# Attention values products: low parts of probabilities against 64 columns of weights, in another order

## The chip, the cores and the metric

The kernel runs on one core of a Trainium2 chip. The metric is the device time of one execution in microseconds (us). A difference under 0.2% (some 3 us here) can't be told from none.

Five engines work side by side: TensorE (PE, whose weight loads the profile shows apart as PEld), VectorE (DVE), ScalarE (ACT), GpSimd (POOL) and SyncE (SP, which issues most transfers).

## The reference

Two token sequences, of 2048 and of 512 tokens with 1024 channels, each go through one attention layer, one Fourier mixing layer and a last normalisation, in float32. Only the end of the attention layer matters here. For each block of 128 queries, with the keys of the block itself and of its two neighbours and a band of 128 to either side:

```
scores = jnp.where(mask, q @ k / 8 + bias, -inf)
p = jnp.exp(scores - m)
denom = jnp.sum(p, -1) + jnp.exp(sink - m)
o = (p / denom) @ v
```

There are 16 heads of 64 channels in 4 groups. Four heads share one group's keys and values.

## The kernel before

Each operand of a product is held as a high part (float32 rounded to a shorter mantissa, `fp32r` in the profile) and a low part (what is left), and a product a·b is made as high·high, high·low and low·high.

The work is in five chunks of 512 tokens (chunk 0 is the short sequence, chunks 1 to 4 the long one). Each chunk makes its keys and values, and then goes through 8 pairs of heads. In it, queries, gates and the output projection of the pairs are made between the attention steps of other pairs, in an order written out by hand: the tables `PERIOD` (chunks 1 to 4) and `FIRST` (chunk 0). Each table is one period, and a period handles two query blocks of one head pair. All TensorE instructions of this stage are chained into that one order.

Names that matter:

- `S1`, `S2` (line 650): scores of a block into the PSUM tiles `spt`. `T0`, `T1` (line 709): transposes of the normalised probabilities into `tp`.
- `hi0`, `hi1` (line 722, ACT) and `lo0`, `lo1` (line 726, DVE): high and low parts of the transposed probabilities, into the tile `pts`. Its second index tells the part: 0 is high, 1 is low.
- `AV1`, `AV2` (lines 759 to 770, function `half`): the values products, into the PSUM tile `av`, one bank for each of the two query blocks. The weights are the values `v`: 128 columns, 64 of the high part and then 64 of the low part. The moving operand is `pts`. So the upper 64 partitions of `av` get what the low parts of the values give, and the lower 64 what the high parts give. `t2` (line 787) copies the upper 64, `add` (line 797) adds them to the lower.

The keys of a block are split in an upper and a lower half of 64 rows, and each half is a product of its own: 64 rows of TensorE's array, 128 columns. `half` issues one product for rows 0 to 63 and one for rows 64 to 127 in turn. The two go to different banks, and TensorE runs them beside each other. In `AV1` rows 0 to 63 work for the first block and rows 64 to 127 for the second, in `AV2` the other way round. Between the two stand the transposes `T0`. `AV2` waits, by an instruction made in `swapped` (line 526), until the other rows are done with its bank.

What a half of the rows does for one block is listed in `reached` (line 741): three key blocks (0 the one before, 1 the block itself, 2 the one behind) times two parts. Of one of the outer key blocks (`edge`) these 64 keys reach only 64 of the 128 queries because of the band, so that product has 2x64 moving columns: a narrow product. The others have 256 (two heads of 128 queries): wide products. At the ends of a sequence a key block is missing, and so are its products. The last two blocks of a chunk's last head pair go another way (line 775) that the change doesn't touch.

Of the kernel before, what the change touches and what calls it, by code (L numbers as in the profile page):

```python
# [20 lines left out]
P = 128  # L21
# [34 lines left out]
def encoder(  # L56
# [17 lines left out]
    av = spsum.tile([P, 2, 512], F32, name="av")  # L74
# [126 lines left out]
    def pe(ins):  # L201
        return seq(PE, ins) if PE in chain else ins

    def attention_phase():

        with ExitStack() as es:
# [167 lines left out]
            vblk, k_splits = {}, []  # L374
# [151 lines left out]
            def swapped(places):  # L526

                before = []
                for last, h in places:
                    if last[1 - h] is not None:  # L530
                        before.append(last[1 - h])
                        last[1 - h] = None
                if before:
                    wait = pe(PE.nop())
                    for ins in before:
                        tc.add_manual_dep(wait.ins, ins.ins.name, DONE, reason="other rows of a bank")
# [73 lines left out]
            def attention(c, p, res, uTs):  # L610

                tok, lo_t, hi_t = CHUNKS[c]
                g = p // 2
# [24 lines left out]
                def span(b):  # L638
                    gb = tok // P + b
                    k0 = 1 if tok + b * P == lo_t else 0  # L640
                    k1 = 2 if tok + (b + 1) * P == hi_t else 3
                    return gb, k0, k1
# [85 lines left out]
                def values(b):  # L728

                    pts = st.pop("pts")  # L730
                    products, last = [], [[None, None], [None, None]]
                    for i in range(2):
                        gb, k0, k1 = span(b + i)
                        for kb in range(k0, k1):
                            v = vblk[gb - 1 + kb][:, g].rearrange("p a d -> p (a d)")
                            for part in range(2):
                                pt = pts[:, part, i, kb].rearrange("p h q -> p (h q)")
                                products.append((i, v, pt))
                    by_block = [[m for m in products if m[0] == i] for i in range(2)]

                    def reached(i, h):

                        gb, k0, k1 = span(b + i)
                        edge, far = 2 * h, 2 - 2 * h
                        order = [(1, 0), (edge, 0), (far, 0), (far, 1), (edge, 1), (1, 1)]
                        rows = ahead = slice(64 * h, 64 * h + 64)
                        out = []
                        for kb, part in order:
                            if k0 <= kb < k1:
                                v = vblk[gb - 1 + kb][rows, g].rearrange("p a d -> p (a d)")  # L750
                                pt = pts[rows, part, i, kb].rearrange("p h q -> p (h q)")
                                to = av[:, i, :256]
                                if kb == edge:
                                    pt = pts[rows, part, i, kb][:, :, ahead]
                                    to = to.rearrange("p (h q) -> p h q", h=2)[:, :, ahead]
                                out.append((i, to, v, pt))
                        return out

                    def half(swap):
                        todo = [reached(h ^ swap, h) for h in range(2)]  # L760
                        if swap:
                            swapped([(last[1], 0), (last[0], 1)])
                        for n in range(max(map(len, todo))):
                            for h in range(2):
                                if n < len(todo[h]):
                                    i, to, v, pt = todo[h][n]
                                    last[i][h] = pe(PE.matmul(  # L767
                                        to, v, pt, start=not swap and n == 0,
                                        stop=swap and n == len(todo[h]) - 1, skip_group_check=True,
                                    ))  # L770

                    def whole():
                        for i, todo in enumerate(by_block):
                            for n, (_, v, pt) in enumerate(todo):
                                pe(PE.matmul(
                                    av[:, i, :256], v, pt, start=n == 0, stop=n == len(todo) - 1, skip_group_check=True
                                ))

                    st["half"] = half
                    return whole  # L780
# [298 lines left out]
            for c in range(len(CHUNKS)):  # L1079
# [89 lines left out]
                for n in range(19):  # L1169
# [12 lines left out]
                    order = [a for a in (PERIOD if c else FIRST) if n < 15 or a[0] not in ("hi0", "lo0")]  # L1182
# [1110 lines left out]
```

## Time and profile before

| | us |
|---|---|
| runs, median of 3 | 1558.24 (1558.18 to 1559.84) |
| the profiled execution, its own time | 1559.2 |
| its span, first to last instruction | 1557.4 |
| TensorE busy (matmul records) | 1540.8, 13150 instructions |
| VectorE busy | 1126.1 |
| ScalarE busy | 889.8 |
| mean granted TensorE clock | 0.998 |

How to read it: a matmul's record lasts from where it is taken up to the modelled end of its results, so records of successive matmuls overlap. What a product costs is the distance from its start to the next start on the same rows. A record that is longer than others of its shape tells that the matmul was taken up and then had to wait, for its weights for example. Weight loads (PEld) run beside matmuls. In a row such as `64*128 64x256`, the first pair is active rows times columns of the array, the second the moving operand; a weight load has its weights there. "xN" merges N successive instructions of one kind. A wait is put down to what ended it.

### The profile page before, as it was taken

The page shows a single profiled execution, that of the slowest core. Times are in us where ns is not written, and L with a number is a line of the kernel's source. Part 1 is how long each engine was busy: PE and PEld are TensorE (multiplying, and loading weights), DVE is VectorE, ACT ScalarE, POOL GpSimd, SP SyncE. Part 2 cuts the span into 40 slices and gives each one's busy share as a digit, 9 for nine tenths or more (in the row PEclk, how much of TensorE's full clock was granted, in tenths as well). Part 3 has the DMA queues.
Part 4 walks back from the last instruction along what each step waited for, and adds up shares of the span by engine and source line. Part 5 has one row for each costly group of instructions (what it writes and reads, how often), then busy time and mean ns, then how long its engine had stood idle before and what let it go on. Part 6 is the DMA issues. An engine that isn't in the chain of part 4 may idle for free.

```text
span 1557.4 us, 33658 instructions
## 1 busy us (share of the span) xinstructions
PE 1540.8 (99%) x13150; PEld 1344.4 (86%) x13150; DVE 1126.1 (72%) x2431; ACT 889.8 (57%) x1921; POOL 450.9 (29%) x616
## 2 busy tenths in 40 slices
PE   9999999999999999999999999999999999999998
PEld 7899888999898888988888899988888888888886
DVE  5888655777638776367764477767888878989896
ACT  6788634787337784257861477747556564343353
POOL 2566662421414313314214242222122111101100
PEclk9999999999999999999999999999999999999999
DMA  8677687684866766866739666665675669556852
GB/s 313 228 288 234 225 337 281 219 292 160 300 221 218 243 230 204 312 211 196 264 124 363 230 212 233 247 243 197 212 248 188 237 226 411 183 203 259 297 187 95
DMA packets 100729, 372.70 MB, mean 239 GB/s; under 512 B 11235, under 2 KB 22251, under 8 KB 83420
## 3 DMA queue, kind: packets, MB, share of 16 engines
q1 hardware_dynamic: 82716, 297.38, 55.4%
q0 software_dynamic: 16688, 70.04, 11.6%
q10 hardware_dynamic: 1168, 3.15, 0.6%
q8 instruction: 103, 1.69, 0.4%
q14 instruction: 54, 0.44, 0.1%
HBM read 280.06 MB, written 90.47 MB: 238 GB/s over the span
## 4 chain that ended last, share of the span: by engine, by line
PE 89%; DVE 6%; ACT 2%; DMA 2%; issue 1%; POOL 0%; POOLq 0%; DVEq 0%; ACTq 0%; SPq 0%
PE pj L524 27%; PE av L767 7%; PE W L134 6%; PE pj L134 6%; PE tp L134 5%; PE av L134 5%; PE spt L650 5%; PE spt L134 4%; PE tp L709 4%; PE Wo L134 3%; PE fo L134 3%; PE Z L134 3%; PE z L1402 2%; PE Zo L134 2%; PE ABp L134 1%; PE X L134 1%
## 5 line engine op out<-in xcount | busy, mean ns | idle before, releaser
L524 PE MATMUL pj<-h,wg 64*128 64x512 f32 x1920 | 438.6, 389 | 0.0
L524 PE MATMUL pj<-h,wq 64*128 64x512 f32 x1560 | 378.8, 389 | 1.3 <-DVE qab L568 1.3
L524 PEld LDWEIGHTS pj<-h,wg 64*128 64x128 f32 x1920 | 330.6, 184 | 23.8
L524 PEld LDWEIGHTS pj<-h,wq 64*128 64x128 f32 x1560 | 284.4, 184 | 21.5 <-DVE qab L568 2.7
L669 DVE CUSTOM_DVE_ANT_0 S<-spt,b 128x385 f32<-128x385 f32 (+1 forms) x320 | 165.0, 525 | 89.2 <-PE spt L650 86.1
L677 ACT ACTIVATE S<-S 128x385 f32<-128x385 f32 (+1 forms) x320 | 189.3, 592 | 62.9 <-DVE S L669 42.5
L722 ACT CAST pts<-tp 128x768 fp32r<-128x768 f32 (+1 forms) x160 | 121.2, 758 | 91.8 <-PE av L767 57.5
L726 DVE TENSOR_TENSOR pts<-tp,pts 128x768 fp32r<-128x768 f32 (+1 forms) x160 | 144.1, 900 | 13.1 <-ACT pts L722 12.3
L767 PE MATMUL av<-pts,v 64*128 64x256 f32 (+1 forms) x1680 | 140.9, 284 | 2.3 <-DVE pts L726 2.3
L767 PEld LDWEIGHTS av<-pts,v 64*128 64x128 f32 x1680 | 125.3, 186 | 6.8 <-DVE pts L726 2.9
L812 POOL TENSOR_TENSOR uT<-o,uT 128x256 fp32r<-128x256 f32 x75 | 56.7, 756 | 241.0 <-ACT uT L808 240.8
L650 PE MATMUL spt<-kwin,qab 64*128 64x384 f32 (+1 forms) x960 | 121.1, 338 | 0.9 <-DVE S L669 0.7
L134 PE MATMUL fo<-wo,tTu 128*128 128x512 f32 x480 | 114.3, 392 | 0.0
L134 PEld LDWEIGHTS fo<-wo,tTu 128*128 128x128 f32 x480 | 88.4, 188 | 17.8
L709 PEld LDWEIGHTS tp<-ident,S 64*128 64x128 f32 x1792 | 91.2, 137 | 10.5 <-DVE pts L726 3.2
L709 PE MATMUL tp<-ident,S 64*128 64x64 f32 x1792 | 96.2, 223 | 0.2 <-DVE pts L726 0.2
L803 POOL TENSOR_TENSOR o<-o,s 128x256 f32<-128x256 f32 x75 | 55.9, 745 | 120.6 <-DVE o L797 94.9
L692 DVE TENSOR_SCALAR S<-S 128x384 f32<-128x384 f32 (+1 forms) x192 | 89.6, 496 | 0.1
L650 PEld LDWEIGHTS spt<-kwin,qab 64*128 64x128 f32 x960 | 85.0, 187 | 3.8 <-issue 1.8
L279 DVE SCALAR_TENSOR_TENSOR h<-xk,g0s,h 128x512 fp32r<-128x512 f32 x40 | 46.6, 1176 | 51.6 <-ACT h L278 51.6
L524 PE MATMUL pj<-wo,uT 64*128 64x512 f32 x360 | 74.8, 390 | 0.0
L278 ACT ACTIVATE h<-xk,g0s 128x512 fp32r<-128x512 f32 x40 | 28.7, 725 | 77.1 <-POOL xk L274 76.4
(376 smaller groups left out, 3357.1 us busy)
## 6 DMA issues: line engine op xcount, KB each, us to landing
wo<-wsd SPq DMA_DIRECT2D x32, 1024.0 KB, 5.4
wq<-wsd SPq DMA_DIRECT2D x31, 1024.0 KB, 6.5
wg<-wsd SPq DMA_DIRECT2D x31, 1024.0 KB, 5.7
x<-x1d SPq DMA_DIRECT2D x40, 512.0 KB, 3.9
b<-b21d SPq DMA_DIRECT2D x40, 512.0 KB, 4.4
b<-rowd SPq DMA_DIRECT2D x40, 384.0 KB, 4.3
xs<-in_x_dram SPq DMA_DIRECT2D x23, 512.0 KB, 6.0
s2d<-gt POOLq DMA_DIRECT2D x40, 256.0 KB, 4.2
```

The lines of the kernel that those rows point to most:

```text
L134: ins = pe(PE.matmul(out, a[i], b[j], start=start and i + j == 0, stop=stop and i == 1, skip_group_check=more))
L524: out.last[h] = pe(PE.matmul(out.ps, a[i], b[j], **out.flags()))
L650: pe(PE.matmul(spt[j][:, 2 + k0 * P : 2 + k1 * P], res["q"][rows, qp, b * P : (b + 1) * P], kwin[g][rows, kp, b * P + k0 * P : b * P + k1 ...
L669: seq(DVE, DVE.tensor_tensor_reduce(out=s[:, e0:e1], in0=ps[:, 1 + e0 : 1 + e1], in1=st["bias"][:, j, 386 - e1 : 386 - e0][:, ::-1], scale ...
L677: last_exp[0] = seq(ACT, ACT.activation(s[:, e0:e1], s[:, e0:e1], AF.Exp, bias=s[:, 386:387], scale=-1.0, accum_out=s[:, 387:388]))
L692: seq(DVE, DVE.tensor_scalar(s[:, ks], s[:, ks], den, None, ALU.mult))
L709: pe(PE.transpose(ps[h][:, kb, j, :], s[rows, j, 1 + kb * P : 1 + (kb + 1) * P], ident[rows, rows]))
L722: seq(ACT, ACT.copy(hi, ps))
L726: seq(DVE, DVE.tensor_tensor(lo, ps, f32(hi), ALU.subtract))
L767: last[i][h] = pe(PE.matmul(to, v, pt, start=not swap and n == 0, stop=swap and n == len(todo[h]) - 1, skip_group_check=True,))
L803: eng.tensor_tensor(o, o, s, ALU.mult)
L812: low = eng.tensor_tensor(lo, o, f32(hi), ALU.subtract)
```

## The change

Two lines in `reached` narrow the products of the low parts of the probabilities (part 1): they take the first 64 columns of `v`, its high part, and write the lower 64 partitions of `av` alone. The product low·low is so no longer made. A third line changes the order of a row half's products. The build turns products with 64 columns of weights into instructions for an array tile of 64 rows by 64 columns, where their neighbours have 64 by 128.

```diff
-                        order = [(1, 0), (edge, 0), (far, 0), (far, 1), (edge, 1), (1, 1)]
+                        order = [(1, 0), (far, 0), (edge, 0), (1, 1), (edge, 1), (far, 1)]
...
-                                v = vblk[gb - 1 + kb][rows, g].rearrange("p a d -> p (a d)")
+                                v = vblk[gb - 1 + kb][rows, g, : 2 - part].rearrange("p a d -> p (a d)")
                                 pt = pts[rows, part, i, kb].rearrange("p h q -> p (h q)")
-                                to = av[:, i, :256]
+                                to = av[: P // (1 + part), i, :256]
```

In entries (key block, part): 1 is the block itself, `edge` is narrow, `far` is the other outer block.

The first place is TensorE's order in an `AV1` in the inner part of a chunk (chunk 2, the third and fourth block of the second head pair), before. The rows of the two halves alternate; a shape is columns of weights times moving columns, so 2x64 is a narrow product; the name after `v` begins with the key block's number.

```order
L767 MATMUL av<-pts_1_2_6981,v_6_6368 128x256
L767 MATMUL av<-pts_1_2_6981,v_7_6371 128x256
L767 MATMUL av<-pts_1_2_6981,v_5_6365 128x2x64
L767 MATMUL av<-pts_1_2_6981,v_8_6374 128x2x64
L767 MATMUL av<-pts_1_2_6981,v_7_6371 128x256
L767 MATMUL av<-pts_1_2_6981,v_6_6368 128x256
L767 MATMUL av<-pts_1_2_6981,v_7_6371 128x256
L767 MATMUL av<-pts_1_2_6981,v_6_6368 128x256
L767 MATMUL av<-pts_1_2_6981,v_5_6365 128x2x64
L767 MATMUL av<-pts_1_2_6981,v_8_6374 128x2x64
L767 MATMUL av<-pts_1_2_6981,v_6_6368 128x256
L767 MATMUL av<-pts_1_2_6981,v_7_6371 128x256
```

The same place of TensorE's order after the change ("x2" merges two successive rows that read alike):

```order
L767 MATMUL av<-pts_1_2_6981,v_6_6368 128x256
L767 MATMUL av<-pts_1_2_6981,v_7_6371 128x256 x2
L767 MATMUL av<-pts_1_2_6981,v_6_6368 128x256
L767 MATMUL av<-pts_1_2_6981,v_5_6365 128x2x64
L767 MATMUL av<-pts_1_2_6981,v_8_6374 128x2x64
L767 MATMUL av<-pts_1_2_6981,v_6_6368 64x256
L767 MATMUL av<-pts_1_2_6981,v_7_6371 64x256
L767 MATMUL av<-pts_1_2_6981,v_5_6365 64x2x64
L767 MATMUL av<-pts_1_2_6981,v_8_6374 64x2x64
L767 MATMUL av<-pts_1_2_6981,v_7_6371 64x256
L767 MATMUL av<-pts_1_2_6981,v_6_6368 64x256
```

The first narrow pair moved one place back, and the last six products have 64 columns of weights. Before, each narrow product stood ahead of a product with 128 columns of weights; now each stands ahead of one with 64.

The second place is TensorE's order in an `AV1` at the start of the long sequence (chunk 1, first blocks of the third head pair), where the first block has no key block ahead of it, before:

```order
L767 MATMUL av<-pts_2_0_4217,v_0_3430 128x256
L767 MATMUL av<-pts_2_0_4217,v_1_3433 128x256 x2
L767 MATMUL av<-pts_2_0_4217,v_2_3436 128x2x64
L767 MATMUL av<-pts_2_0_4217,v_1_3433 128x256
L767 MATMUL av<-pts_2_0_4217,v_0_3430 128x256 x3
L767 MATMUL av<-pts_2_0_4217,v_2_3436 128x2x64
L767 MATMUL av<-pts_2_0_4217,v_1_3433 128x256
```

And after:

```order
L767 MATMUL av<-pts_2_0_4217,v_0_3430 128x256
L767 MATMUL av<-pts_2_0_4217,v_1_3433 128x256 x2
L767 MATMUL av<-pts_2_0_4217,v_0_3430 128x256
L767 MATMUL av<-pts_2_0_4217,v_0_3430 64x256
L767 MATMUL av<-pts_2_0_4217,v_2_3436 128x2x64
L767 MATMUL av<-pts_2_0_4217,v_1_3433 64x256 x2
L767 MATMUL av<-pts_2_0_4217,v_2_3436 64x2x64
L767 MATMUL av<-pts_2_0_4217,v_0_3430 64x256
```

Here the two halves have different numbers of products, and one half's product with 64 columns stands ahead of the other half's last product with 128. The instructions of the other engines keep their order.

## The prediction

> **What bounds the kernel now.** I read the page first, for the engine that paces the kernel and the chain of work that ended last.
>
> ```profile
> span 1557.4 us, 33658 instructions
> ...
> PE 1540.8 (99%) x13150; PEld 1344.4 (86%) x13150; DVE 1126.1 (72%) x2431; ACT 889.8 (57%) x1921; POOL 450.9 (29%) x616
> ...
> PE 89%; DVE 6%; ACT 2%; DMA 2%; issue 1%; POOL 0%; POOLq 0%; DVEq 0%; ACTq 0%; SPq 0%
> ```
>
> TensorE is in 89% of the chain. What is taken from it is taken from the time as long as nobody else becomes late. Next I read whom it waits for in the attention stage (the view of waits, PE alone, 39 to 1015 us), and how busy the others are there (one inner chunk, 475 to 597 us).
>
> ```profile
> PE av L767 <- DVE pts L726: 2.3, 2, 1.2
> PE pj L524 <- DVE qab L568: 1.3, 4, 0.4
> PE spt L650 <- DVE S L669: 0.7, 2, 0.4
> PE tp L709 <- DVE pts L726: 0.2, 1, 0.2
> ...
> 475.02:597.04 122.02, 121.66 (x1497) 106.77 (x1494) 93.63 (x252) 94.76 (x216) 35.71 (x48) 1.00 0.66 220
> ```
>
> The columns of the last row are the stretch, its length, and the busy time of PE, PEld, DVE, ACT and POOL. In all the attention TensorE waits 4.5 us for others, 2.3 us of it ahead of a values product. VectorE is busy 93.63 of 122.02 us (77%), ScalarE about as much. So the change is weighed on TensorE alone.
>
> Third, groups of instructions by shape: the wide and the narrow values products, a product of the same wide shape elsewhere, and the loads of weights.
>
> ```profile
> L767 PE MATMUL av<-pts,v 64*128 64x256 f32 x1140 | 140.9, 314 | 2.3 <-DVE pts L726 2.3
> ...
> L767 PE MATMUL av<-pts,v 64*128 64x128 f32 x540 | 72.9, 222 | 0.0
> ...
> L650 PE MATMUL spt<-kwin,qab 64*128 64x256 f32 x192 | 22.2, 281 | 0.0
> ...
> L767 PEld LDWEIGHTS av<-pts,v 64*128 64x128 f32 x1680 | 125.3, 186 | 6.8 <-DVE pts L726 2.9 <-issue 0.2
> ...
> L356 PEld LDWEIGHTS pj<-ohr,rbs 33*16 33x16 f32 x2 | 0.1, 90 | 0.4 <-issue 0.4
> ```
>
> A wide values product lasts 314 ns on average where a score product of the same shape lasts 281. Something holds up many of the 1140. The timeline shows what, where another line's rows keep the records apart, with the record of the second product in ns:
>
> ```profile
> 302.94 0.22 PE L767 MATMUL av<-pts,v 64*128 64x128 f32 x1
> 302.99 0.22 PE L709 MATMUL tp<-ident,S 64*128 64x64 f32 x1
> 303.00 0.33 PE L767 MATMUL av<-pts,v 64*128 64x256 f32 x1
> ...
> L767 PE MATMUL av<-pts,v x1: 332/332/332, 303.0 to 303.0; 64*128 64x256 f32 x1
> ```
>
> A narrow product starts at 302.94 (in chunk 1). The wide product behind it on the same rows is taken up 0.06 us later, so 60 ns is what the narrow one needs for its moving columns. But the wide record lasts 332 ns, 51 more than the 281 of its shape (55 more than 277, the median of line 767's records in the inner chunk, below). I read these 55 ns as a wait for its 128 columns of weights, whose load can't hide behind 60 ns. So a narrow product costs 115 ns, not 60.
>
> ```profile
> L767 PE MATMUL av<-pts,v x337: 217/277/360, 475.0 to 597.0; 64*128 64x256 f32 x113, 64*128 64x128 f32 x56
> ```
>
> **The change part by part.** *Fewer columns of weights.* The load rows give the price of a column: 186 ns for 128 columns, 90 ns for 16, so 96 / 112 = 0.86 ns each. A load of 64 columns is then 186 - 64 x 0.86 = 131 ns, 55 shorter. That is just what was exposed: behind a narrow product nothing would be left of the wait. Behind a wide product a load hides already, and there 64 columns save nothing. Moving columns stay as they were.
>
> *The order.* It decides which loads stand behind narrow products. In TensorE's order of before all 540 narrow products are followed on their own rows by a values product with 128 columns of weights, 510 by a wide and 30 by a narrow one. After the change 510 are followed by a wide product with 64 columns, and the other 30 (at sequence ends) by the next step's with 128. So 510 waits of 55 ns go and about 30 stay. Two halves of the rows run beside each other: 510 / 2 x 55 ns = 14.0 us.
>
> The bounds of this term: an `AV1` or `AV2` with all key blocks has two narrow products in each half, so it gains 2 x 55 = 110 ns. There are 150 of these (5 chunks, 8 head pairs, 4 each, less the two of each chunk that go the other way), and where a block lacks a neighbour the half with more products, which has both narrow ones, ends last. 150 x 110 ns = 16.5 us if that half alone counts. On the low side 51 ns in place of 55 and a third of it lost to waits that come nearer give 510 / 2 x 51 x 2/3 = 8.7 us. The measured ceiling is the mean: 33 ns x 1140 / 2 = 18.8 us for all that holds up wide values products. I take 14.0 us, the count by halves.
>
> *What comes nearer.* The low products of `AV1` wait for `lo1`. Ahead of the first of them stand two wide and one narrow product, as before, but the last now costs no wait, so they start some 55 ns sooner. The row of waits shows 2 waits there in the whole stage, so I cost this at nothing; if that cover were gone, 75 `AV1` times 55 ns is 4 us. `AV2` waits for the other rows' last product of `AV1`, and `T0` covers that:
>
> ```profile
> 501.44 0.86 PE L767 MATMUL av<-pts,v 64*128 64x256 f32 x12
> 502.13 0.53 PE L709 MATMUL tp<-ident,S 64*128 64x64 f32 x12
> 502.48 0.94 PE L767 MATMUL av<-pts,v 64*128 64x256 f32 x12
> 503.26 0.69 PE L650 MATMUL spt<-kwin,qab 64*128 64x384 f32 x6
> ```
>
> `AV1` starts at 501.44 and its records end at 502.30; `AV2` begins at 502.48. The last product stays a wide one, so this distance of 0.18 us stays. `AV1` takes 0.69 us up to `T0` and `AV2` 0.78 us up to the scores; each should lose 0.11.
>
> *Less behind the product.* The low·low part is gone from the upper 64 partitions of `av`; `t2` and `add` read the same shapes as before and cost the same. Their start follows `AV2`.
>
> *The sum.* The profiled execution took 1559.2 us (span 1557.4 and 1.8 around it): 1559.2 - 14.0 = 1545.2, which I round to 1545. That execution was 1 us over the median of the runs, 1558.24; against the median the same sum gives 1544.
>
> **What the new shape may cost.** The instructions with 64 columns are made for another tile of the array. What a change of shape costs, the trace shows for rows:
>
> ```profile
> 38.62 1.07 PE L134 MATMUL pj<-h,wq 128*128 128x512 f32 x4
> ...
> 39.62 0.41 PEld L650 LDWEIGHTS spt<-kwin,qab 64*128 64x128 f32 x6 [0.35 <-issue]
> 39.62 0.62 PE L650 MATMUL spt<-kwin,qab 64*128 64x256 f32 x6
> ...
> L650 PE MATMUL spt<-kwin,qab x2: 381/381/381, 39.6 to 39.6; 64*128 64x256 f32 x2
> ...
> 17.98 0.84 PE L134 MATMUL spt<-h,wk 128*128 128x512 f32 x3
> 18.75 0.63 PE L356 MATMUL pj<-ohr,rbs 33*16 33x512 f32 x2
> ```
>
> Four full matmuls start at 38.62 and end at 39.69; the records of this shape last 0.39, so the last starts at 39.30, and they step by (39.30 - 38.62) / 3 = 0.23. The first product on 64 rows starts at 39.62, 0.32 later: 0.09 more than a step. The weight loads stood idle 0.35 us, waiting for nothing that the profile shows. And the record is 381 ns, 100 more than 281: the load wasn't made ahead. So a change of rows costs 0.09 + 0.10 = 0.19 us. At 18.75 rows and columns change together (33 rows, 16 columns). The last full matmul starts at 17.98 + 0.84 - 0.39 = 18.43, again 0.32 earlier. Columns added nothing to what rows cost; no row shows columns changing alone.
>
> **The rivals.** *A change of columns costs as much as a change of rows.* TensorE's order has 180 stretches of products with 64 columns, so 180 changes in and 180 out (one each for the 150, and 30 more where the halves are out of step). Out, to 128 columns: 0.19 us. In, to 64: 0.09 and half of 0.10, 0.14 us. 180 x 0.33 = 59 us, less the 14.0 saved: 45 us slower, 1604. If TensorE's 4.5 us of waits vanish in it, 1600; at 0.19 us both ways, 180 x 0.38 - 14.0 = 54 us, 1614. The rival decides as soon as a pair of changes costs more than 14.0 / 180 = 78 ns. For it: the one price in the trace for another shape is 190 ns, some five times the break-even of 39 a change. Against it: all such rows change the rows in use, and the one that changes columns too costs no more, so I read the price as that of the rows. Chance 0.20.
>
> The Trainium skill, page TensorEngine Tiling (Array Packing), section Key Properties, says that a change of tiling mode, not of tile alone, drains TensorE, and the section Available Configurations lists 64x128 and 64x64 as different modes; by that rule the time is the 1604 of this rival. The trace agrees where rows change (0.19 us); for columns alone no run here shows it. The page PSUM — Partial Sum Buffer, section PSUM: the matmul accumulator, says that float32r matmuls force the instruction's column group to all four strips; by that these products would keep their neighbours' mode and 1545 would stand, and no trace here can show that field.
>
> *Nothing to gain.* If the narrow product itself took 115 ns, whatever the weights, or a load of 64 columns were no shorter, the time would stay at 1559.2 (1558 against the median). Against it: the wide product is taken up 60 ns behind the narrow one, and the load of 16 columns is 96 ns shorter. Chance 0.06.
>
> *The gain is given to waits.* `hi0` waits on ScalarE for `AV2`, and comes sooner; no one engine is near its limit at 77%, so I see no place for it beyond the third that the low bound of 8.7 us takes in (1550.5). It is part of the forecast's range.
>
> **How the numbers follow.** The forecast, 1545 with its own range of 1542 to 1551 (16.5 and 8.7 us off, a little rounded), has a chance of 0.74, the slower rival 0.20, no gain 0.06. For 8 in 10 the range takes in the no-gain case and leaves out the slower one: 1541 to 1562. Faster by over 0.2% (3.1 us): 0.74. Within: 0.06. Slower: 0.20.
>
> **What would show it.** In the profile after: wide products of line 767 with a mean near 281 where it was 314; loads `64*64` near 131 ns; the inner `AV1` of 0.69 us at 0.58, `AV2` of 0.78 at 0.67; no idle time of the weight loads by "issue" ahead of line 767. I am wrong if loads ahead of `64*64` products stand idle 0.35 us and an `AV1` grows to 0.9 us, or if the loads are shorter and the steps are not.

## The result, and the profile after

The changed kernel takes 1546.87 us (median, 1545.72 to 1547.23), the kernel before 1558.83 us: a ratio of 0.9911, 95% interval 0.9897 to 0.9926. That is 12.0 us less (11.5 to 16.1 by the interval) where 14 had been forecast, inside the range, and faster by over 0.2%, which had the chance of 0.74. The profiled execution took 1545.72 us, 0.7 from the forecast of 1545. Its span of 1543.2 us is 14.2 shorter than the 1557.4 of before, at the same mean granted clock (0.998). The other three runs after were granted 0.996 to 0.997 and had spans of 1544.2 to 1545.5 us; so a part of the 2 us between 12.0 and 14.2 may go with the clock.

The same lines of the page, after:

```profile
span 1543.2 us, 33658 instructions
...
PE 1525.3 (99%) x13150; PEld 1331.4 (86%) x13150; DVE 1124.2 (73%) x2431; ACT 888.4 (58%) x1921; POOL 451.5 (29%) x616
...
PE 86%; DVE 6%; DMA 4%; ACT 2%; issue 1%; POOL 0%; SPq 0%; POOLq 0%; DVEq 0%; ACTq 0%
```

TensorE paces the kernel as before, with 86% of the chain where it had 89%, and its busy time fell by 15.5 us. The other engines are busy for as long as before, within 2 us. The groups by shape show where it fell: the values products of after, with their loads.

```profile
L767 PE MATMUL av<-pts,v 64*64 64x256 f32 x570 | 75.9, 277 | 2.4 <-DVE pts L726 2.3
...
L767 PE MATMUL av<-pts,v 64*128 64x256 f32 x570 | 69.6, 302 | 0.0
...
L767 PEld LDWEIGHTS av<-pts,v 64*128 64x128 f32 x840 | 71.7, 186 | 4.3 <-ACT S L690 0.4 <-issue 0.2
...
L767 PEld LDWEIGHTS av<-pts,v 64*64 64x64 f32 x840 | 54.8, 132 | 3.1 <-DVE pts L726 3.1
```

A load of 64 columns takes 132 ns (131 had been worked out from the loads of 128 and 16). All wide products behind narrow ones are now among the 570 with 64 columns, whose mean of 277 ns is the shape's own: the 55 ns of waiting are gone. The idle time of the loads by "issue" is 0.2 us, as before. The wide products with 128 columns still have a mean of 302, and that is read below. Counted from these means, the wide records lost (1140 x (314 - 277) - 570 x (302 - 277)) / 2 = 14.0 us, by halves.

The inner `AV1` and `AV2` that the prediction timed, in the timeline after:

```profile
493.93 0.75 PE L767 MATMUL av<-pts,v 64*128 64x256 f32 x12
494.52 0.53 PE L709 MATMUL tp<-ident,S 64*128 64x64 f32 x12
494.87 0.84 PE L767 MATMUL av<-pts,v 64*128 64x256 f32 x12
495.55 0.34 PE L650 MATMUL spt<-kwin,qab 64*128 64x384 f32 x2
```

`AV1` takes 0.59 us up to the transposes (0.69 before) and `AV2` 0.68 up to the scores (0.78): 0.10 less in each, where 0.11 was expected. The same `AV1` in records of line 767 (least, median and longest in ns), in the changed kernel, then in the kernel before:

```profile
L767 PE MATMUL av<-pts,v x12: 217/274/279, 493.9 to 494.4; 64*128 64x256 f32 x4, 64*64 64x256 f32 x4, 64*128 64x128 f32 x2, 64*64 64x128 f32 x2
```

```profile
L767 PE MATMUL av<-pts,v x10: 218/274/332, 501.4 to 501.9; 64*128 64x256 f32 x6, 64*128 64x128 f32 x4
```

No record over 279 ns is left where the longest was 332 (the second row's window misses two of the twelve). No new wait for another engine took the place: TensorE's waits in the attention stage of the changed kernel are those of before. What did move is seen in the score products at the sequence ends (the last row; 281 ns before): 192 x 8 ns are some 28 waits of 55 ns. These fit the 30 narrow products that now stand ahead of the next step's 128 columns.

```profile
PE av L767 <- DVE pts L726: 2.3, 2, 1.2
PE pj L524 <- DVE qab L568: 1.2, 4, 0.4
PE spt L650 <- DVE S L669: 0.7, 2, 0.4
PE tp L709 <- DVE pts L726: 0.2, 1, 0.2
...
L650 PE MATMUL spt<-kwin,qab 64*128 64x256 f32 x192 | 21.9, 289 | 0.0
```

### The profile page after: what moved, and what is told of

Read it like the earlier page. It is cut to its first block, busy times and chain, and to the rows that moved or that the text cites. A ratio compares the mean times of both kernels' runs of the same rounds, so it can differ in the third digit from the quotient of the medians.

```text
span 1543.2 us, 33658 instructions
## 1 busy us (share of the span) xinstructions
PE 1525.3 (99%) x13150; PEld 1331.4 (86%) x13150; DVE 1124.2 (73%) x2431; ACT 888.4 (58%) x1921; POOL 451.5 (29%) x616
## 4 chain that ended last, share of the span: by engine, by line
PE 86%; DVE 6%; DMA 4%; ACT 2%; issue 1%; POOL 0%; SPq 0%; POOLq 0%; DVEq 0%; ACTq 0%
PE pj L524 27%; PE W L134 6%; PE pj L134 6%; PE av L767 6%; PE tp L134 5%; PE av L134 5%; PE spt L650 5%; PE spt L134 4%; PE tp L709 3%; PE Wo L134 3%; PE Z L134 3%; PE fo L134 3%; PE z L1402 2%; PE Zo L134 2%; PE X L134 1%; PE ABp L134 1%
## 5 line engine op out<-in xcount | busy, mean ns | idle before, releaser
L767 PE MATMUL av<-pts,v 64*128 64x256 f32 (+3 forms) x1680 | 123.8, 267 | 2.4 <-DVE pts L726 2.3
L767 PEld LDWEIGHTS av<-pts,v 64*64 64x64 f32 (+1 forms) x1680 | 108.4, 159 | 7.4 <-DVE pts L726 3.1
L709 PEld LDWEIGHTS tp<-ident,S 64*128 64x128 f32 x1792 | 86.6, 138 | 10.7 <-DVE pts L726 3.1
L709 PE MATMUL tp<-ident,S 64*128 64x64 f32 x1792 | 91.1, 223 | 0.2 <-DVE pts L726 0.2
L650 PEld LDWEIGHTS spt<-kwin,qab 64*128 64x128 f32 x960 | 81.5, 186 | 3.8 <-issue 1.8
```

Source lines behind the costliest of these rows:

```text
L650: pe(PE.matmul(spt[j][:, 2 + k0 * P : 2 + k1 * P], res["q"][rows, qp, b * P : (b + 1) * P], kwin[g][rows, kp, b * P + k0 * P : b * P + k1 ...
L709: pe(PE.transpose(ps[h][:, kb, j, :], s[rows, j, 1 + kb * P : 1 + (kb + 1) * P], ident[rows, rows]))
L767: last[i][h] = pe(PE.matmul(to, v, pt, start=not swap and n == 0, stop=swap and n == len(todo[h]) - 1, skip_group_check=True,))
```

## The experiments

The theory to test (A): a load of 128 columns takes too long to hide behind a narrow product, a load of 64 hides, and a change of columns costs nothing. Its rivals: the order alone (B), shorter loads anywhere (C), a small price for each change of columns (D), and the narrower tile as such (F). E comes with the last experiment. The kernel before ran beside each of them, with a median of 1560.91 us on one chip and 1561.39 on another, so the ratios are what compares. A ratio is turned into us by the 1558.83 of the result.

**The order alone.** Against the changed kernel, 128 columns of weights in all products:

```diff
-v = vblk[gb - 1 + kb][rows, g, : 2 - part].rearrange("p a d -> p (a d)")
+v = vblk[gb - 1 + kb][rows, g].rearrange("p a d -> p (a d)")
-to = av[: P // (1 + part), i, :256]
+to = av[:, i, :256]
```

> The new order with 128 columns of weights in all products, so low times low is made again. Theory A (a load of 128 columns can't hide behind a narrow product, a load of 64 can): every narrow product is still followed by 128 columns, all waits of 55 ns stay, the time is that of before, 1558.8 us (1556 to 1561). Rival B (the place of the narrow products is what counts, or the changed order lets the banks or the waits fall better): part or all of the measured gain of 12.0 us, 1547 to 1553.

Measured: 1560.73 us, ratio 0.9998 (0.9988 to 1.0008), no change. Its wide values products are as long as before:

```profile
L767 PE MATMUL av<-pts,v 64*128 64x256 f32 x1140 | 140.7, 314 | 2.4 <-DVE pts L726 2.3
```

The order by itself brings nothing, as theory A has it; rival B falls.

**64 columns alone.** The order of before:

```diff
-order = [(1, 0), (far, 0), (edge, 0), (1, 1), (edge, 1), (far, 1)]
+order = [(1, 0), (edge, 0), (far, 0), (far, 1), (edge, 1), (1, 1)]
```

> 64 columns of weights in the products of the low parts, in the order of before. Theory A: 270 of the 540 narrow products (those of the low parts) stand ahead of 64 columns, and so do 30 of the others at sequence ends; 240 still stand ahead of 128. 300 / 2 x 55 ns = 8.2 us, at the measured rate (12.0 for 14.0) 7.1 us less than before: 1551.7 us (1549.5 to 1553). Rival C (loads of 64 columns help wherever they stand, since they take less of the array's or the memory's time): the whole gain, 1546.9. Rival B (the order): about 1558.8.

Measured: 1553.67 us, ratio 0.9951 (0.9934 to 0.9967): 0.0049 x 1558.83 = 7.6 us less than before (5.1 to 10.3), where 7.1 was expected and rival C had the whole 12.0. The records tell which waits are left:

```profile
L767 PE MATMUL av<-pts,v 64*128 64x256 f32 x570 | 87.0, 323 | 0.0
L767 PE MATMUL av<-pts,v 64*64 64x256 f32 x570 | 77.7, 277 | 2.3 <-DVE pts L726 2.3
```

Wide products with 64 columns wait no more, those with 128 wait more often than in the changed kernel (323 against 302), since 240 of them stand behind narrow ones. Shorter loads help where they stand behind a narrow product, and not wherever they stand; rival C falls. So the order is worth the rest, some 4 to 6 us by the medians, but only with the 64 columns.

**Columns changing from product to product.**

```diff
-order = [(1, 0), (far, 0), (edge, 0), (1, 1), (edge, 1), (far, 1)]
+order = [(1, 0), (1, 1), (far, 0), (far, 1), (edge, 0), (edge, 1)]
```

> Columns change from product to product: each high part's product is followed by the low part's of the same key block. 450 stretches of 64 columns in TensorE's order where the changed kernel has 180. Theory A, with no price on a change of columns: all narrow products of the high parts stand ahead of 64 columns; the narrow low ones at the end of a half stand ahead of transposes (whose loads are short) or, 150 of them, of 128 columns where the changed kernel has 30 of these: 120 / 2 x 55 ns = 3.3 us more than the changed kernel, 1550.2 us (1549 to 1552). Rival D (a change of columns costs something, and the 2 us that the gain fell short of 14 are its price, 11 ns a pair of changes): 270 x 11 ns = 3 us more, 1553.2. At the price that changes of rows show, 0.33 us a pair, 1639.

Measured: 1551.73 us, ratio 0.9937 (0.9919 to 0.9955): 9.8 us less than before, 1549.0 on its scale. Theory A said 1550.2, rival D 1553.2, the price of a change of rows 1639. The last is out by far. The interval (1546.2 to 1551.8) holds A's time and leaves D's just outside, but the runs scattered (1548.55 to 1555.92); the next one tells A from D more surely.

**The disputed cost by itself.** Rows of products on rows 0 to 63 in front of the changed kernel, each set on its own line, all operands of ones, twelve products of each kind:

```diff
+run(12, lambda: PE.matmul(b[:, :128], r[:, :128], r[:, :128], **F))
+run(12, lambda: PE.matmul(b[:96, :128], r[:, :96], r[:, :128], **F))
+run(12, lambda: PE.matmul(b[:64, :128], r[:, :64], r[:, :128], **F))
+run(12, lambda: PE.matmul(b[:32, :128], r[:, :32], r[:, :128], **F))
+run(12, lambda: PE.matmul(b[:, :256], r[:, :128], r[:, :256], **F))
+run(12, lambda: PE.matmul(b[:, :256], r[:, :128], r[:, :256], **F),
+    lambda: PE.matmul(lo, r[:, :64], r[:, :256], **F))
...
+run(12, lambda: PE.matmul(b[:, :256], k[:, :128], k[:, :256], **F),
+    lambda: PE.matmul(lo, k[:, :64], k[:, :256], **F))
+run(12, lambda: PE.matmul(hi, k[:, :64], k[:, :256], **F),
+    lambda: PE.matmul(lo, k[:, :64], k[:, :256], **F))
```

(`r` is fp32r, `k` bf16, `lo` the lower 64 partitions of a bank and `hi` the upper; the dots stand for the set of line 335.)

> The changed kernel with rows of products on 64 rows put in front, whose results nothing uses; read from the trace alone. Products in fp32r with 128 moving columns and 128, 96, 64 or 32 columns of weights, twelve of each: theory A gives steps of 115 ns at 128 columns, 115 - 32 x 0.86 = 87 at 96, 60 at 64 and no less than 60 at 32, since there the moving columns bind. Products in fp32r with 256 moving columns: 117 ns a step with 128 columns; with 128 and 64 in turn 117 as well if a change of columns has no price, and 117 + 78 or more a step if it has one that would have undone the gain; rival D's 11 ns a pair makes 122. The same in bf16: the same steps if the shape of the tile never mattered by its columns; some 190 ns more a step if it does in that form.

Measured, in the timeline: narrow products with 128, 96, 64 and 32 columns (lines 328 to 331), twelve in each row; then, in ns, the records of the first set and the loads of two sets.

```profile
11.28 1.55 PE L328 MATMUL pj<-probe 64*128 64x128 f32 x12
12.67 1.19 PE L329 MATMUL pj<-probe 64*96 64x128 f32 x12
13.70 0.88 PE L330 MATMUL pj<-probe 64*64 64x128 f32 x12
14.41 0.88 PE L331 MATMUL pj<-probe 64*32 64x128 f32 x12
...
L328 PE MATMUL pj<-probe x12: 268/272/325, 11.3 to 12.6; 64*128 64x128 f32 x12
...
L329 PEld LDWEIGHTS pj<-probe x12: 162/162/162, 12.6 to 13.5; 64*96 64x96 f32 x12
...
L331 PEld LDWEIGHTS pj<-probe x12: 104/105/110, 14.4 to 15.0; 64*32 64x32 f32 x12
```

A row's length less the record of its last product (0.27, 0.25, 0.22, 0.22 us), by 11 steps: 116, 85, 60 and 60 ns a step. The first set holds one record of 325 ns, 53 over its median of 272; without these 53 ns its step is 112. 115, 87, 60 and 60 were expected. In this trace the narrow product is bound by its load down to some 64 columns (the step falls from 112 to 60 ns), by its moving columns below (60 at 64 and at 32).

Then wide products in fp32r with 128 and 64 columns in turn (lines 333 and 334), the first and the last of 24 rows and five between them:

```profile
16.63 0.28 PE L333 MATMUL pj<-probe 64*128 64x256 f32 x1
...
17.35 0.28 PE L333 MATMUL pj<-probe 64*128 64x256 f32 x1
17.47 0.28 PE L334 MATMUL pj<-probe 64*64 64x256 f32 x1
17.59 0.28 PE L333 MATMUL pj<-probe 64*128 64x256 f32 x1
17.71 0.28 PE L334 MATMUL pj<-probe 64*64 64x256 f32 x1
17.82 0.28 PE L333 MATMUL pj<-probe 64*128 64x256 f32 x1
...
19.39 0.28 PE L334 MATMUL pj<-probe 64*64 64x256 f32 x1
```

23 steps take 19.39 - 16.63 = 2.76 us, 120 ns each. Twelve products with 128 columns alone:

```profile
15.14 1.65 PE L332 MATMUL pj<-probe 64*128 64x256 f32 x12
```

(1.65 - 0.28) / 11 = 0.125, with one record in it that is 53 ns longer than the others (333 against 280); without these 53 ns a step is 120 ns here too. A change between 128 and 64 columns costs nothing in fp32r, where rival D had 5.5 ns a change; rival D falls, and with it the slower rival. The same in bf16, alone (line 335) and in turn (336 and 337):

```profile
19.51 1.51 PE L335 MATMUL pj<-const-bfloat16-1.0 64*128 64x256 bf16 x12
20.86 0.27 PE L336 MATMUL pj<-const-bfloat16-1.0 64*128 64x256 bf16 x1
21.07 0.29 PE L337 MATMUL pj<-const-bfloat16-1.0 64*64 64x256 bf16 x1
21.29 0.28 PE L336 MATMUL pj<-const-bfloat16-1.0 64*128 64x256 bf16 x1
21.50 0.29 PE L337 MATMUL pj<-const-bfloat16-1.0 64*64 64x256 bf16 x1
```

Alone a step is (1.51 - 0.27) / 11 = 0.11 us; in turn it is (21.50 - 20.86) / 3 = 0.21. So in bf16 each change between the two shapes costs 0.10 us. The loads tell that more than the tile changes there:

```profile
L336 PEld LDWEIGHTS <-const-bfloat16-1.0 x12: 92/93/103, 20.8 to 26.3; 64*128 64x128 bf16 x12
L337 PEld LDWEIGHTS <-const-bfloat16-1.0 x12: 101/103/124, 21.1 to 26.7; 64*64 64x64 bf16 x12
```

In bf16 the load of 128 columns (93 ns) is shorter than that of 64 (103 ns), where in fp32r it is longer (186 and 132). Whether the 0.10 us go with the tile or with the kind of load was not tried.

The Trainium skill, page TensorEngine Tiling (Array Packing), section Key Properties, says that a change of tiling mode drains TensorE. For fp32r the measurement differs (120 ns a step with and without the change) and decides; for bf16 the trace fits it (0.21 against 0.11 us) without showing the cause. The Trainium skill's page PSUM — Partial Sum Buffer, section PSUM: the matmul accumulator, has it that float32r matmuls force the column group; that could explain the difference, and no run here shows that field.

**96 columns.** Fewer columns to load, but the tile of 64 by 128:

```diff
+v = vblk[gb - 1 + kb][rows, g].rearrange("p a d -> p (a d)")[:, : P - 32 * part]
+to = av[: P - 32 * part, i, :256]
```

> The changed kernel with 96 columns of weights in the low parts' products, in place of 64 (part of low times low is made again). The build makes these for a tile of 64 rows by 128 columns, so the shape of the tile never changes. Theory A (only the number of columns to load counts): of each wait of 55 ns 32 x 0.86 = 27.5 stay, so half of the gain: 6 us less than before, 1552.8 us (1551 to 1554.5), and wide products behind narrow ones with records near 305 ns. Rival F (the gain comes with the narrower tile, not with the columns): no gain, 1558.8.

Measured: 1551.41 us, ratio 0.9939 (0.9924 to 0.9954). The changed kernel, run again beside it:

> The changed kernel itself, beside the others on one chip: 0.9911 of the kernel before (0.990 to 0.9925), for the step from here to the version that puts a low part's product first behind the transposes.

Measured: 1547.84 us, ratio 0.9915 (0.9900 to 0.9930). In the records half of the wait is left:

```profile
L767 PE MATMUL av<-pts,v 64*96 64x256 f32 x570 | 84.2, 300 | 2.4 <-DVE pts L726 2.3
...
L767 PEld LDWEIGHTS av<-pts,v 64*96 64x96 f32 x840 | 63.5, 160 | 3.0 <-DVE pts L726 3.0
```

510 of these 570 stand behind a narrow one, so (300 - 277) x 570 / 510 = 26 ns of wait for each, where 27.5 was expected. Rival F falls: the columns count, the tile doesn't. By the ratio the gain is 9.5 us against 13.3, more than the half (6 us) that was written down: 1549.3 on the scale of the result, below the expected 1551 to 1554.5. By spans at the same mean clock of 0.998 (1548.8, 1543.2 and 1557.4 us) it is 8.6 of 14.2. The trace accounts for 510 / 2 x (55 - 26) = 7.4 us. What the rest is, stays open; the interval reaches down to 0.0046 x 1558.83 = 7.2.

**A low product first, behind the transposes.** The wide products with 128 columns kept a mean of 302 ns in the changed kernel. The rows for the start of the inner `AV2` tell why; the changed kernel:

```profile
L767 PEld LDWEIGHTS av<-pts,v x2: 194/194/194, 494.8 to 494.8; 64*128 64x128 f32 x2
L767 PE MATMUL av<-pts,v x2: 362/362/362, 494.9 to 494.9; 64*128 64x256 f32 x2
```

The first product of `AV2` is 85 ns too long (362 against 277; 360 in the kernel before). It stands behind transposes that step by some 62 ns ((0.53 - 0.22) us over 5 steps of a row half). So:

```diff
 order = [(1, 0), (far, 0), (edge, 0), (1, 1), (edge, 1), (far, 1)]
+if i != h:
+    order = [(1, 1), (1, 0), (far, 0), (edge, 0), (edge, 1), (far, 1)]
```

> The second half-step of the values products begins with a low part's product with 64 columns, right behind the transposes, and each narrow product still stands ahead of 64 columns. In the changed kernel the first product there has a record of 362 ns against 277 of its shape, 85 too long. Theory A: that is a wait for 128 columns behind a transpose that takes 62 ns; 64 columns take 55 ns off in each of 75 such steps, 4.1 us: 1542.8 us (1541.5 to 1544.5). Rival E (the 85 ns are the wait until the other rows are done with the bank): 1546.9, as the changed kernel.

Measured: 1542.28 us, ratio 0.9877 (0.9856 to 0.9897), 1539.7 on the scale of the result and so below the expected 1541.5 to 1544.5. Run again beside the changed kernel:

> The version with a low part's product first behind the transposes, beside the changed kernel on one chip: 4.1 us less than it by theory A (3 to 5.5); the same as it by rival E.

Measured: 1542.20 us, ratio 0.9884 (0.9866 to 0.9903), 0.0031 x 1558.83 = 4.8 us less than the changed kernel beside it (0.9915); 4.1 was expected. The record at the same place, and the wide products with 128 columns:

```profile
L769 PE MATMUL av<-pts,v x2: 309/309/309, 492.9 to 492.9; 64*64 64x256 f32 x2
...
L769 PE MATMUL av<-pts,v 64*128 64x256 f32 x570 | 62.9, 278 | 0.0
L769 PE MATMUL av<-pts,v 64*64 64x256 f32 x570 | 86.9, 288 | 2.4 <-DVE pts L726 2.3
```

53 of the 85 ns are gone, where 55 were expected: the mean with 128 columns fell from 302 to 278, while that with 64, which now come first, rose from 277 to 288. By these records the step is worth (24 - 11) x 570 / 2 = 3.7 us. The theory, found on narrow products, holds behind transposes too, and rival E falls for the 53 ns. The other 32 ns fit an estimate from the probe: 128 moving columns take 60 ns a step, so the 64 of a transpose some 30, and loads that step by 112 and 60 ns would show by 82 and 30 behind it. No run tests that. This version was faster than the changed kernel in both comparisons, though the intervals of the two just meet (0.9903 and 0.9900), so the size of the step is rough.

## Why the prediction was right

- **What bounds the kernel.** TensorE does, and what its waits for weights gave up came off the span of the profiled execution in full: 14.2 us, where the term of the sum was 510 / 2 x 55 ns = 14.0 and the records lost 14.0. That the two agree within 0.2 us is in part luck: by the medians the gain was 12.0 us, and 13.3 when it was run again.
- **The 55 ns are a wait for weights.** Read from one record of 332 ns behind a narrow product. The order alone (all loads long, no gain), 96 columns (26 ns left) and the sets of narrow products (112, 85 and 60 ns a step) show it.
- **The price of a column,** 0.86 ns from loads of 128 and 16 columns, gave 131 ns for 64 and 158 for 96; measured were 132 and 160 to 162.
- **What comes nearer.** Nothing: no wait for another engine grew, and the slack ahead of the low products and of `AV2` held, as costed (`AV2` still begins 0.19 us behind the end of `AV1`'s records). The 30 waits that were to stay are seen on the score products.
- **The slower rival** fell in this kernel: a change of columns in fp32r costs nothing. The reading from the row at 18.75 us (rows and columns together cost no more than rows) was right, though it could not show columns alone, so this was a judgment and not a reading. A chance of 0.20 was not too much: in bf16 the price is 0.10 us a change, more than twice the 0.039 at which the rival would have decided.
- **Mis-sized.** "Wide products of line 767 with a mean near 281" held for those with 64 columns alone (277). The others kept 302, since the step of the prediction that gave all of the excess to narrow products left out the first product of `AV2`. Its 75 x 85 ns = 6.4 us were in the ceiling of 18.8 us and in no term; the prediction's own row of the inner chunk has such a record as its longest (360). The last experiment took 53 of the 85 ns.
- The two bounds for how the halves add up (14.0 by the mean of both, 16.5 if one alone counts) lie just below and well above the 14.2 us, and both medians are below 14; the mean was the better count.

## What to carry to other kernels

When TensorE is busy all the time, look for matmuls whose record is longer than others of their shape: each may hide a wait, often for weights behind a product too short to hide their load. Compare the load's step with the moving time of the product ahead of it, put short loads behind short products and long ones behind long products, and make weights narrower where part of them isn't needed. Before adding a new shape of tile, measure what the change costs in the very number format that is used.

## What was not expected of the hardware

- A change between 128 and 64 columns of weights costs 0.10 us in bf16 and nothing in fp32r, in the same trace, on the same rows. Which columns are used doesn't matter by itself: the probe's last set (lines 338 and 339), for which nothing had been forecast, has 64 columns throughout, in bf16, in the upper and the lower half of a bank in turn.

```profile
26.88 0.42 PE L339 MATMUL pj<-const-bfloat16-1.0 64*64 64x256 bf16 x1
...
29.23 0.42 PE L339 MATMUL pj<-const-bfloat16-1.0 64*64 64x256 bf16 x1
```

A pair takes (29.23 - 26.88) / 11 = 0.21 us there at a granted clock of 0.50. By an estimate from the 0.11 us at 1.00, one product of 256 moving columns would need about that alone (0.22 us): so the two run beside each other, and at that clock nothing is seen to be lost between them.
- In the bf16 set that changes columns TensorE stayed at the granted clock of 1.00 for the first 3.4 us and was then at 0.50, through the set behind it too (each row: the stretch, its length, the engines' busy time, the granted clock, DMA):

```profile
20.87:24.30 3.43, 3.43 (x18) 1.47 (x15) 1.61 (x4) 1.28 (x3) 1.05 (x1) 1.00 1.03 420
24.40:29.20 4.80, 4.80 (x32) 2.79 (x32) 0.00 (x0) 0.00 (x0) 0.00 (x0) 0.50 1.03 420
```

By its records TensorE was busy all the time in both stretches. Why the clock fell was not tried.
